# Scan of a two-block transformer kernel: exclusive cumulative sum by subtraction, transposes a step behind, weights of the later modulation scaled and added on VectorE

## The chip, the cores and the metric

The kernel runs on one core of one Trainium2 chip. A core has five engines with a queue each: TensorE (PE, with PEld for its weight loads), VectorE (DVE), ScalarE (ACT), GpSimd (POOL) and SyncE (SP), which issues most DMAs. The metric is device time in microseconds from start to end; smaller is better.

## The reference, cut to what matters

```python
def reference(...):                                   # one layer of block one, two of block two
    m_x = split(silu(c) @ mod_w + mod_b, 6)           # modulation: shifts, scales and gates, 6 x 1024
    h_x = modulate(rms_norm(x, norm1_g), m_x[0], m_x[1]);  h_c = ...           # latent and context, 256 tokens each
    z = h @ w_in                                      # r, k, v, low ranks, q, k, v, two gates
    ya = rwkv_mixer(z_c, z_x, ...)                    # the scan: both directions, 8 heads of 64
    yb = na_mixer(z_c, z_x, ...)                      # neighbourhood attention
    x = x + m_x[2] * branch_merge(z_x[9], z_x[10], ya, yb, proj_a, proj_b, w_out)
    x = x + m_x[5] * moe(modulate(rms_norm(x, norm2_g), m_x[3], m_x[4]), ...)  # 16 experts, 2 a token
    return second_block(x, ...)                       # two layers: mixer, feed-forward, gate

def rwkv_prep(...):                                   # what a step of the scan needs
    wl = w0 + tanh(lw) @ w_lora_b                     # log-decay, from a low rank
    decay = exp(-exp(-softplus(-wl) - 0.5))
    a = sigmoid(a0 + la @ a_lora_b)
    kk = normalised(k * k_k);  k_dir = k * (1 + (a - 1) * k_a)

def step(s, (w_t, k_t, v_t, kk_t, a_t, r_t)):         # over 256 context, then 256 latent tokens
    s = s * w_t - (s @ kk_t) outer (kk_t * a_t) + v_t outer k_t
    y = s @ r_t
```

## The kernel before

The work lies in stages one behind the other: norm and the first part of the modulation, input products with neighbourhood attention, the scan, the merge of both branches, the experts, and the two layers of the second block. The change is in the scan and in two things that are done beside it.

**The scan** (`rwkv`) is done in chunks of 128 tokens. Two directions, two groups of four heads and four chunks make 16 units. Three slots (`SLOTS`) take them in turn, so that slot 0 has six units and the others five. Each unit is a generator: `rwkv_prep` makes the rows of the chunk, `rwkv_chunk` makes the masked products of a chunk and calls `solve` for the triangular solve, then the state and the output are updated. Each `yield` ends a step. The function `turns` goes round all live generators and takes one step of each: three slots (each a few steps apart), `gates` (products of the gates, 160 steps), `factors` with `modulation_rest` and `bonus`, and `rwkv_out`. This round is the order in which the code is written; a scheduler then sets the order within each engine's queue, with that order as priority. Each engine takes its queue strictly from the front.

**The preparation of a unit** (`rwkv_prep`) writes `th` (tanh of decay and a), makes cumulative sums of the decay over the tokens with two products against masks of zeros and ones (`cum["i"]`, inclusive, L669; `cum["e"]`, exclusive, L670), takes exponentials of them on ACT (`pe` from the exclusive sum, `pinv` and `pi` from the inclusive one), and multiplies on DVE into the rows `rr` (L688), `nb` (L698, L699), `kh` (L703 to L705) and, in the latent chunks, `pi` (L709). `turn` transposes such a row on PE (L686, two transposes of 128x128) and copies it with ACT to `krT` or `nkT` (L687). The first use of the transposed rows is L735. The products of the solve are L835, L841 and L844, with copies `nt` on ACT (L830) and masked products `x` on DVE (L837).

**The later modulation** (`modulation_rest`): for eight blocks of 512 columns, eight pieces of `mod_w` (128x512, 256 KB each) come by DMA into `mr` (three buffers). ACT scales each with its column of silu(c) (L300), POOL adds it to `mra` (L302), and PE sums `mra` over the partitions with a column of ones (L307). Two steps lie behind each piece. DVE also makes the low parts `wl` of the gates' weights (L128).

Of the kernel before, what the change touches and what calls it, by code (L numbers as in the profile page):

```python
# [12 lines left out]
AF = mybir.ActivationFunctionType  # L13
ALU = mybir.AluOpType
# [57 lines left out]
class Kernel:  # L72
# [212 lines left out]
    def modulation_rest(self, pool):  # L285

        nc, a = self.nc, self.a
        self.rw = self.gp.tile([P, 8, 16], F32, name="rw")
        self.rbh = self.keep.tile([P, 16], F32, name="rb")
        nc.sync.dma_start(self.rw, a["router_w"].rearrange("(k p) e -> p k e", p=P))  # L290
        rb = a["router_bias"]
        nc.sync.dma_start(self.rbh, bass.AP(tensor=rb.tensor, offset=rb.offset, ap=[[0, P], [1, 16]]))
        nc.vector.tensor_scalar(self.rbh, self.rbh, 0.5, None, op0=ALU.add)
        w = a["mod_w"][0]
        for q in range(4, 12):
            acc = pool.tile([P, 512], F32, tag="mra", name="mra", bufs=1)
            for k in range(8):
                raw = pool.tile([P, 512], F32, tag="mr", name="mr", bufs=3)
                nc.sync.dma_start(raw, w[k * P:(k + 1) * P, q * 512:(q + 1) * 512])
                nc.scalar.activation(raw if k else acc, raw, AF.Copy, scale=self.sc[:, k, 0:1])  # L300
                if k:
                    nc.gpsimd.tensor_tensor(acc, acc, raw, op=ALU.add)  # L302
                yield
                yield
            ps = self.bank()
            for j in range(4):
                nc.tensor.matmul(ps[:, j:j + 1], acc[:, j * P:(j + 1) * P], self.ones, start=True, stop=True)  # L307
            nc.vector.tensor_tensor(self.m[:, q * 4:q * 4 + 4, 0], ps[:, 0:4], self.col["mod_b"][:, q * 4:q * 4 + 4],
                                    op=ALU.add)
            yield  # L310

        self.fac = self.keep.tile([P, 32], F32, name="fac")
        nc.vector.tensor_scalar(self.fac[:, 0:8], self.m[:, 16:24, 0], 0.5, None, op0=ALU.mult)
        nc.vector.tensor_copy(self.fac[:, 24:32], self.m[:, 40:48, 0])
        nc.vector.scalar_tensor_tensor(self.fac[:, 8:16], self.m[:, 32:40, 0], 1.0, self.col["norm2_g"], op0=ALU.add,
                                       op1=ALU.mult)
        nc.vector.tensor_copy(self.fac[:, 16:24], self.m[:, 24:32, 0])
        ps = self.bank()
        nc.tensor.transpose(ps[0:32, 0:P], self.fac, self.ident)
        row = pool.tile([32, P], F32, tag="mra", name="frow", bufs=1)  # L320
        nc.vector.tensor_copy(row, ps[0:32, 0:P])
        self.facrow = self.dram.tile([32, P], F32, name="facrow")
        nc.sync.dma_start(self.facrow[:, :], row)
# [163 lines left out]
    def rwkv_constants(self):  # L487
        nc, c, a = self.nc, self.rc, self.a
# [9 lines left out]
        f = lambda n: cell[0].tile([P, P], F32, name=n)  # L498
        tt, ts = nc.vector.tensor_tensor, nc.vector.tensor_scalar
        w0, w1, w2 = f("w0"), f("w1"), f("w2")  # L500
        wi0, wi1 = c.tile([P, P], I32, name="wi0"), c.tile([P, P], I32, name="wi1")
        pf, sf = f("pf"), f("sf")
# [2 lines left out]
        ts(sf, si, 0.0, None, op0=ALU.add)  # L505

        self.cum = {}
        for d, (ge_i, ge_e, half) in enumerate(((ALU.is_ge, ALU.is_gt, ALU.is_lt), (ALU.is_le, ALU.is_lt, ALU.is_ge))):
            ts(w0, pf, 64.0, None, op0=half)
            for kind, op in (("i", ge_i), ("e", ge_e)):  # L510
                m = f(f"cum{kind}{d}")
                tt(m, sf, pf, op=op)
                tt(m, m, w0, op=ALU.subtract)
                self.cum[kind, d] = m

        self.off = c.tile([P, 8], F32, name="off")
        self.offn = c.tile([P, 8], F32, name="offn")
# [10 lines left out]
        for d, (st, inc) in enumerate(((ALU.is_gt, ALU.is_ge), (ALU.is_lt, ALU.is_le))):  # L528
            m = c.tile([P, 4, P], F16, name=f"mk4{d}")
# [5 lines left out]
        for k in range(6):  # L535
# [5 lines left out]
            for d in range(2):  # L541
                m = (pf, sf)[d]
# [99 lines left out]
    def rwkv_prep(self, s, d, g, t, cur, first):  # L642

        nc, pool = self.nc, self.rp
        mm = nc.tensor.matmul
        tt, stt = nc.vector.tensor_tensor, nc.vector.scalar_tensor_tensor
# [5 lines left out]
        flat = lambda ap: ap.rearrange("p a b -> p (a b)")  # L652
# [7 lines left out]
        thw, tha = th[:, 0:256], th[:, 256:512]  # L660
# [6 lines left out]

        bi = self.bank()
        mm(bi[:, 0:256], self.cum["i", d], thw, start=True, stop=True)  # L669
        mm(bi[:, 256:512], self.cum["e", d], thw, start=True, stop=True)  # L670
        pinv, pe = tmp("pinv"), tmp("pe")
        h = -0.5 * CDEC
        nc.scalar.activation(pe, bi[:, 256:512], AF.Exp, scale=h, bias=self.off[:, 2 * d + 1:2 * d + 2])
        nc.scalar.activation(pinv, bi[:, 0:256], AF.Exp, scale=-h, bias=self.offn[:, 2 * d:2 * d + 1])
        if emit:
            pi = tmp("pi")
# [3 lines left out]
        rr, nb, kh = own([P, 2, 4, 64], "rr"), own([P, 256], "nb"), own([P, 256], "kh")  # L680
        krT, nkT = own([P, 2, 2, P], "krT"), own([P, 2, 2, P], "z0")

        def turn(src, dst):
            b = self.bank()
            for p in range(2):
                nc.tensor.transpose(b[:, p * P:(p + 1) * P], src[:, p * P:(p + 1) * P], self.ident)  # L686
            nc.scalar.activation(dst, b[:, 0:256].rearrange("p (a t) -> p a t", a=2), AF.Copy)  # L687
        tt(flat(rr[:, 0]), kk, pe, op=ALU.mult)  # L688
        turn(flat(rr[:, 0]), krT[:, :, 0, :])

        bt = self.bank()
        for p in range(2):
# [1 line left out]
        hv = self.sm.tile([P, 2, 2], F32, tag=f"hv{s}", name="hv", bufs=2)  # L694
        nc.scalar.activation(hv, bt[:, 0:4].rearrange("p (a b) -> p a b", b=2), AF.Exp, scale=h, bias=self.off64)
        yield
        u = tmp("t0")
        stt(u, tha, 1.0, kk, op0=ALU.add, op1=ALU.mult)  # L698
        stt(nb, u, -0.5, pinv, op0=ALU.mult, op1=ALU.mult)  # L699
        turn(nb, nkT[:, 0])  # L700
        yield
        u = tmp("t0")
        stt(u, tha, -1.0, self.kab[:, fs], op0=ALU.add, op1=ALU.mult)  # L703
        stt(u, u, 1.0, self.zk[t][:, fs], op0=ALU.add, op1=ALU.mult)
        tt(kh, u, pinv, op=ALU.mult)  # L705
        turn(kh, nkT[:, 1])
        yield
        if emit:
            tt(pi, self.zr[t][:, fs], pi, op=ALU.mult)  # L709
            turn(pi, krT[:, :, 1, :])  # L710
            yield
        cur.update(hv=hv, rr=rr, nb=nb, kh=kh, krT=krT, nkT=nkT)

    def rwkv_chunk(self, s, d, g, t, cur, state, i, y):
# [1520 lines left out]
```

## Time and profile before

| | |
|---|---|
| time, median of 3 runs | 1558.77 us (1555.15 to 1559.71) |
| the profiled execution | 1560.86 us |
| its span | 1559.1 us |
| PE, PEld busy | 1471.2 us (94%), 1122.8 us (72%) |
| DVE, ACT, POOL busy | 867.1 us (56%), 673.0 us (43%), 197.4 us (13%) |

Busy times are those of the span. The profiled execution is one of its own, and its time is a little above the median of the others. Lines such as L302 are lines of the kernel before.

### The profile page before, as it was taken

Reading aid. Unit: us, or ns where it says so; the run is one execution under the profiler, and the core shown is the slowest. Engines: PE = TensorE matmul, PEld = TensorE weight load, DVE = VectorE, ACT = ScalarE, POOL = GpSimd, SP = SyncE. Lnnn points to the kernel's source line nnn. Section 1 sums busy time; section 2 is a strip of 40 time slices with the busy share of each in tenths; the row PEclk is TensorE's granted clock in tenths of the full one; section 3 lists DMA queues with packets and bytes.
Section 4 is the critical chain, followed back from the end, with each engine's and each line's share of the span. In section 5 each row is a group of like instructions: output and inputs, shape, how many; then the busy total and the mean of one; then the engine's idle time right before and its main releaser. Section 6 shows DMA issues by size and latency. Waiting matters only on the chain.

```text
span 1559.1 us, 26053 instructions
## 1 busy us (share of the span) xinstructions
PE 1471.2 (94%) x10562; PEld 1122.8 (72%) x10562; DVE 867.1 (56%) x1826; ACT 673.0 (43%) x1097; POOL 197.4 (13%) x253
## 2 busy tenths in 40 slices
PE   5899999989999999789999899999999999999996
PEld 3677777878777777644443358699988887998885
DVE  3678547676666776522211245564556755755555
ACT  2433556665556553210110145554444545544443
POOL 1001123332233510058000000000000000000000
PEclk9899998898899999889999999999999999999999
DMA  9412223221222234779999925355556453555542
GB/s 326 158 46 68 68 84 116 82 82 56 68 82 83 82 119 154 306 308 420 420 419 420 393 85 187 109 188 182 181 182 202 146 189 96 175 189 189 189 162 75
DMA packets 119175, 276.29 MB, mean 177 GB/s; under 512 B 8672, under 2 KB 31876, under 8 KB 107784
## 3 DMA queue, kind: packets, MB, share of 16 engines
q1 hardware_dynamic: 115608, 270.13, 49.4%
q10 hardware_dynamic: 3407, 4.42, 0.8%
q8 instruction: 85, 1.39, 0.4%
q14 instruction: 43, 0.34, 0.1%
q0 software_dynamic: 32, 0.00, 0.0%
HBM read 272.41 MB, written 2.11 MB: 176 GB/s over the span
## 4 chain that ended last, share of the span: by engine, by line
PE 54%; DVE 1%; ACT 1%; issue 0%; DVEq 0%; ACTq 0%
PE mm L119 12%; PE mm L120 12%; PE mm L121 12%; PE mm L1546 11%; PE mm L1531 1%; PE mm L1694 1%; PE mm L1610 1%; PE mm L1951 1%; PE mm L1970 1%; PE mm L1812 1%; PE mm L1924 0%; PE mm L1980 0%; PE mm L217 0%; DVE wl L184 0%; PE mm L1913 0%
## 5 line engine op out<-in xcount | busy, mean ns | idle before, releaser
L184 DVE TENSOR_TENSOR wl<-wr,wh 128x2048 fp32r<-128x2048 f32 (+2 forms) x128 | 269.1, 2103 | 206.7 <-ACT wh L183 194.2
L183 ACT ACTIVATE wh<-wr 128x2048 fp32r<-128x2048 f32 (+2 forms) x128 | 224.9, 1760 | 156.3 <-PE mm L121 105.5
L121 PE MATMUL mm<-xTh,wl 128*128 128x256 f32 x512 | 143.9, 281 | 0.0
L120 PE MATMUL mm<-xTl,wh 128*128 128x256 f32 x512 | 143.7, 281 | 0.0
L119 PE MATMUL mm<-xTh,wh 128*128 128x256 f32 x512 | 143.3, 281 | 0.0
L119 PE MATMUL mm<-wh,fh 128*128 128x512 f32 x256 | 101.4, 396 | 0.0
L121 PE MATMUL mm<-wh,fl 128*128 128x512 f32 x256 | 101.1, 395 | 0.0
L120 PE MATMUL mm<-wl,fh 128*128 128x512 f32 x256 | 101.0, 395 | 0.0
L120 PEld LDWEIGHTS mm<-xTl,wh 128*128 128x128 f32 x512 | 96.2, 188 | 0.9 <-DVE xTl L968 0.3
L119 PEld LDWEIGHTS mm<-xTh,wh 128*128 128x128 f32 x512 | 96.1, 188 | 0.7
L119 PE MATMUL mm<-wh,xTh 128*128 128x512 f32 (+1 forms) x272 | 95.8, 352 | 0.6 <-ACT big L1888 0.4
L121 PEld LDWEIGHTS mm<-xTh,wl 128*128 128x128 f32 x512 | 96.4, 188 | 0.0
L120 PE MATMUL mm<-wl,xTh 128*128 128x512 f32 (+1 forms) x272 | 92.8, 342 | 0.0
L121 PE MATMUL mm<-wh,xTl 128*128 128x512 f32 (+1 forms) x272 | 92.6, 342 | 0.0
L302 POOL TENSOR_TENSOR mra<-mra,mr 128x512 f32<-128x512 f32 x56 | 74.3, 1327 | 54.5 <-ACT mr L300 29.6
L830 ACT ACTIVATE nt<-mm 128x512 f16<-128x512 f32 x80 | 47.2, 593 | 43.9 <-PE mm L844 38.0
L119 PEld LDWEIGHTS mm<-wh,xTh 128*128 128x128 f32 x272 | 51.2, 188 | 8.4 <-issue 0.7
L967 ACT ACTIVATE yh<-hu 128x512 fp32r<-128x512 f32 x16 | 10.1, 630 | 109.0 <-DVE hu L1602 93.8
L121 PEld LDWEIGHTS mm<-wh,fl 128*128 128x128 f32 x256 | 48.1, 188 | 11.5
L119 PE MATMUL mm<-hlh,wh 128*128 128x256 f32 x152 | 56.1, 369 | 0.0
L120 PEld LDWEIGHTS mm<-wl,fh 128*128 128x128 f32 x256 | 48.1, 188 | 10.8
L119 PEld LDWEIGHTS mm<-wh,fh 128*128 128x128 f32 x256 | 48.1, 188 | 10.7
(576 smaller groups left out, 3512.1 us busy)
## 6 DMA issues: line engine op xcount, KB each, us to landing
wr<-in_w_up_dram SPq DMA_DIRECT2D x32, 1024.0 KB, 5.7
wr<-in_w_down_dram SPq DMA_DIRECT2D x32, 1024.0 KB, 5.0
wr<-in_w_in_dram SPq DMA_DIRECT2D x22, 1024.0 KB, 5.2
wr<-in_moe_w_dram SPq DMA_DIRECT2D x21, 1024.0 KB, 13.5
wh<-in_moe_w_dram SPq DMA_DIRECT2D x20, 1024.0 KB, 13.4
wl<-in_moe_w_dram SPq DMA_DIRECT2D x20, 1024.0 KB, 14.3
mr<-in_mod_w_dram SPq DMA_DIRECT2D x64, 256.0 KB, 2.9
wx<-in_moe_w_dram SPq DMA_DIRECT2D x14, 1024.0 KB, 12.8
```

Source lines behind the costliest of these rows:

```text
L119: mm(out, l.hi, r.hi, start=start, stop=False, **kw)
L120: mm(out, l.hi, r.lo, start=False, stop=False, **kw)
L121: mm(out, l.lo, r.hi, start=False, stop=stop, **kw)
L183: self.nc.scalar.activation(w.hi, raw, AF.Copy)
L184: self.nc.vector.tensor_tensor(w.lo, raw, w.hi.bitcast(F32), op=ALU.subtract)
L302: nc.gpsimd.tensor_tensor(acc, acc, raw, op=ALU.add)
L830: nc.scalar.activation(nt, v4(bz), AF.Copy)
L1531: mm(b[:, k * 256:k * 256 + 256], part[:, t, 2 * q + k, :], sel[:, t].rearrange("p j c -> p (j c)"), start=(i == 0), stop=(i == 3))
L1546: mm(b[r], lT[:, k0 + k, c0 + SLOT * j:c0 + SLOT * j + SLOT], w[:, k], start=(start and k == 0), stop=(stop and k == n - 1))
L1610: mm(acc[2 * n + k // 2][:, k % 2], part[:, k * P:(k + 1) * P], back, start=False, stop=(g == 7 and part is y.lo), skip_group_check=True)
L1694: mm(banks[t], first[:, k, t * P:(t + 1) * P], w[:, k, :], start=(k == 0), stop=False)
L1812: nc.tensor.transpose(b[:, j * P:(j + 1) * P], self.x[:, t, 512 * n + j * P:512 * n + (j + 1) * P], self.ident)
```

## The change

Three edits. The masks of the exclusive sum and its product go; the exclusive sum of a token is the inclusive one less the token's own value, so `pe` is now the inclusive product's result minus `thw`, on DVE, and the exponential is taken in place. Each transpose (`turn`) stands one step behind the step that makes its row, and the preparation of a unit yields once more (six steps and not five; in latent chunks seven and not six). In `modulation_rest`, DVE scales a piece and adds it in one instruction; the first piece of a block is still scaled by ACT.

```diff
--- before.py
+++ after.py
@@ -297,9 +297,10 @@
             for k in range(8):
                 raw = pool.tile([P, 512], F32, tag="mr", name="mr", bufs=3)
                 nc.sync.dma_start(raw, w[k * P:(k + 1) * P, q * 512:(q + 1) * 512])
-                nc.scalar.activation(raw if k else acc, raw, AF.Copy, scale=self.sc[:, k, 0:1])
                 if k:
-                    nc.gpsimd.tensor_tensor(acc, acc, raw, op=ALU.add)
+                    nc.vector.scalar_tensor_tensor(acc, raw, self.sc[:, k, 0:1], acc, op0=ALU.mult, op1=ALU.add)
+                else:
+                    nc.scalar.activation(acc, raw, AF.Copy, scale=self.sc[:, k, 0:1])
                 yield
                 yield
             ps = self.bank()
@@ -505,13 +506,11 @@
         ts(sf, si, 0.0, None, op0=ALU.add)
 
         self.cum = {}
-        for d, (ge_i, ge_e, half) in enumerate(((ALU.is_ge, ALU.is_gt, ALU.is_lt), (ALU.is_le, ALU.is_lt, ALU.is_ge))):
+        for d, (ge_i, half) in enumerate(((ALU.is_ge, ALU.is_lt), (ALU.is_le, ALU.is_ge))):
             ts(w0, pf, 64.0, None, op0=half)
-            for kind, op in (("i", ge_i), ("e", ge_e)):
-                m = f(f"cum{kind}{d}")
-                tt(m, sf, pf, op=op)
-                tt(m, m, w0, op=ALU.subtract)
-                self.cum[kind, d] = m
+            m = self.cum["i", d] = f(f"cumi{d}")
+            tt(m, sf, pf, op=ge_i)
+            tt(m, m, w0, op=ALU.subtract)
 
         self.off = c.tile([P, 8], F32, name="off")
         self.offn = c.tile([P, 8], F32, name="offn")
@@ -667,10 +666,10 @@
 
         bi = self.bank()
         mm(bi[:, 0:256], self.cum["i", d], thw, start=True, stop=True)
-        mm(bi[:, 256:512], self.cum["e", d], thw, start=True, stop=True)
         pinv, pe = tmp("pinv"), tmp("pe")
         h = -0.5 * CDEC
-        nc.scalar.activation(pe, bi[:, 256:512], AF.Exp, scale=h, bias=self.off[:, 2 * d + 1:2 * d + 2])
+        tt(pe, bi[:, 0:256], thw, op=ALU.subtract)
+        nc.scalar.activation(pe, pe, AF.Exp, scale=h, bias=self.off[:, 2 * d + 1:2 * d + 2])
         nc.scalar.activation(pinv, bi[:, 0:256], AF.Exp, scale=-h, bias=self.offn[:, 2 * d:2 * d + 1])
         if emit:
             pi = tmp("pi")
@@ -686,7 +685,6 @@
                 nc.tensor.transpose(b[:, p * P:(p + 1) * P], src[:, p * P:(p + 1) * P], self.ident)
             nc.scalar.activation(dst, b[:, 0:256].rearrange("p (a t) -> p a t", a=2), AF.Copy)
         tt(flat(rr[:, 0]), kk, pe, op=ALU.mult)
-        turn(flat(rr[:, 0]), krT[:, :, 0, :])
 
         bt = self.bank()
         for p in range(2):
@@ -694,21 +692,24 @@
         hv = self.sm.tile([P, 2, 2], F32, tag=f"hv{s}", name="hv", bufs=2)
         nc.scalar.activation(hv, bt[:, 0:4].rearrange("p (a b) -> p a b", b=2), AF.Exp, scale=h, bias=self.off64)
         yield
+
+        turn(flat(rr[:, 0]), krT[:, :, 0, :])
         u = tmp("t0")
         stt(u, tha, 1.0, kk, op0=ALU.add, op1=ALU.mult)
         stt(nb, u, -0.5, pinv, op0=ALU.mult, op1=ALU.mult)
+        yield
         turn(nb, nkT[:, 0])
-        yield
         u = tmp("t0")
         stt(u, tha, -1.0, self.kab[:, fs], op0=ALU.add, op1=ALU.mult)
         stt(u, u, 1.0, self.zk[t][:, fs], op0=ALU.add, op1=ALU.mult)
         tt(kh, u, pinv, op=ALU.mult)
+        yield
         turn(kh, nkT[:, 1])
-        yield
         if emit:
             tt(pi, self.zr[t][:, fs], pi, op=ALU.mult)
+            yield
             turn(pi, krT[:, :, 1, :])
-            yield
+        yield
         cur.update(hv=hv, rr=rr, nb=nb, kh=kh, krT=krT, nkT=nkT)
 
     def rwkv_chunk(self, s, d, g, t, cur, state, i, y):
```

The scheduler's order changes from shortly before the scan to its end, on all engines. Behind it, the instructions stand in the same order as before. The lines of the kernel after lie one or two off those of the kernel before.

DVE's queue of the kernel before, in the seventh unit, from its row `rr` to the low part of the next gate weights:

```order
L688 TENSOR_TENSOR rr_3996<-kk,pe 128x256
L699 SCALAR_TENSOR_TENSOR nb_3997<-t_4037,pinv 128x256
L703 SCALAR_TENSOR_TENSOR t_4077<-th,kab 128x256
L704 SCALAR_TENSOR_TENSOR t_4077<-t_4077,zk 128x256
L837 TENSOR_TENSOR x_4026<-mm,lv_1173 128x256
L705 TENSOR_TENSOR kh_3998<-t_4077,pinv 128x256
L128 TENSOR_TENSOR wl<-wr,wh 128x512
```

The preparation's five instructions stand almost side by side, with one product of the solve between. The modulation's additions are on POOL and not in this queue.

The same place in the kernel after, from the subtraction that makes `pe`:

```order
L671 TENSOR_TENSOR pe<-mm,th 128x256
L854 CAST x_3922<-mm 64x256
L301 SCALAR_TENSOR_TENSOR mra<-mr,silu_c,mra 128x512
L687 TENSOR_TENSOR rr_3984<-kk,pe 128x256
L838 TENSOR_TENSOR x_4010<-mm,lv_1167 128x256
L699 SCALAR_TENSOR_TENSOR nb_3985<-t_4019,pinv 128x256
L301 SCALAR_TENSOR_TENSOR mra<-mr,silu_c,mra 128x512
L703 SCALAR_TENSOR_TENSOR t_4058<-th,kab 128x256
L301 SCALAR_TENSOR_TENSOR mra<-mr,silu_c,mra 128x512
L872 TENSOR_TENSOR rr_3247<-rr_3247,mm 128x512
L704 SCALAR_TENSOR_TENSOR t_4058<-t_4058,zk 128x256
```

Three instructions of L301, the scaled additions, now stand in this queue between `pe` and the row `kh` (L705, two rows further on), and two instructions stand between `pe` and `rr`.

PE's queue of the kernel before, at the transpose of the same unit's row `rr` (L693 is the sum over the halves of the chunk):

```order
L119 MATMUL mm<-hlh,wh 128x256
L120 MATMUL mm<-hll,wh 128x256
L121 MATMUL mm<-hlh,wl 128x256
L119 MATMUL mm<-hlh,wh 128x256
L686 MATMUL mm<-ident,rr_3996 128x128 x2
L693 MATMUL mm<-half,th 128x2 x2
L862 LDWEIGHTS x_3933
L862 MATMUL mm<-nt_3932,x_3933 64x64
```

The transpose and the sum over the halves stand side by side.

PE's queue of the kernel after, at the sum over the halves (here L691), and then at the transpose of `rr` (here L685):

```order
L845 LDWEIGHTS x_3934
L845 MATMUL mm<-nt_3888,x_3934 64x64
L120 MATMUL mm<-hll,wh 128x256
L121 MATMUL mm<-hlh,wl 128x256
L691 MATMUL mm<-half,th 128x2 x2
L119 MATMUL mm<-hlh,wh 128x256
L120 MATMUL mm<-hll,wh 128x256
L121 MATMUL mm<-hlh,wl 128x256
L863 LDWEIGHTS x_3922
```

```order
L119 MATMUL mm<-hlh,wh 128x256
L120 MATMUL mm<-hll,wh 128x256
L121 MATMUL mm<-hlh,wl 128x256
L119 MATMUL mm<-hlh,wh 128x256
L120 MATMUL mm<-hll,wh 128x256
L685 MATMUL mm<-ident,rr_3984 128x128 x2
L870 MATMUL mm<-rq_3466,tT_2094 128x128 x4
L842 LDWEIGHTS nt_3976
L842 MATMUL mm<-x_4010,nt_3976 64x64
```

The sum has kept its place behind the solve's products, and the transpose has moved back behind the next step's solve products (L863, L836) and gate products (L119 to L121): some twenty products stand between the two.

## Rows read from the trace of the kernel before

**Rows 1.** Windows: busy us (x instructions) of PE, PEld, DVE, ACT, POOL; clock, DMA share, GB/s.

```profile
0.00:220.00 220.00, 196.71 (x1137) 144.01 (x1137) 133.80 (x485) 88.74 (x168) 16.11 (x29) 0.95 0.35 118
220.00:600.00 380.00, 353.70 (x4194) 294.57 (x4194) 256.78 (x542) 216.21 (x455) 125.93 (x133) 0.92 0.32 95
600.00:1559.00 959.00, 920.81 (x5233) 684.17 (x5232) 476.54 (x801) 368.05 (x475) 55.32 (x91) 0.98 0.62 223
```

**Rows 2.** Waits of PE, 222 to 600 us: total us, times, longest.

```profile
PE mm L686 <- DVE kh L705: 8.1, 8, 1.9
PE mm L841 <- DVE x L837: 3.3, 5, 1.6
PE mm L686 <- DVE rr L688: 2.3, 5, 0.8
PE mm L686 <- DVE nb L699: 0.4, 1, 0.4
```

**Rows 3.** Groups of POOL, 220 to 600 us: count | busy us, mean ns | idle before.

```profile
L302 POOL TENSOR_TENSOR mra<-mra,mr 128x512 f32<-128x512 f32 x56 | 74.3, 1327 | 54.5 <-ACT mr L300 29.6 <-ACT mra L300 17.4 <-PE mm L852 5.7
```

**Rows 4.** Groups of ACT, 220 to 620 us.

```profile
L300 ACT ACTIVATE mr<-mr,silu_c 128x512 f32<-128x512 f32 x56 | 39.7, 718 | 20.2 <-DMA mr<-in_mod_w_dram 18.7 <-POOL mra L302 1.5
```

**Rows 5.** Groups of PE, 222 to 600 us.

```profile
L670 PE MATMUL mm<-th,cume 128*128 128x256 f32 x32 | 9.6, 382 | 0.0
```

**Rows 6.** Groups of DVE, 220 to 620 us.

```profile
L128 DVE TENSOR_TENSOR wl<-wr,wh 128x512 fp32r<-128x512 f32 x48 | 37.3, 776 | 16.4 <-ACT wh L127 15.3 <-ACT mr L300 0.7 <-issue 0.2
L703 DVE SCALAR_TENSOR_TENSOR t<-th,kab 128x256 f32<-128x256 f32 x16 | 10.6, 664 | 0.1
L699 DVE SCALAR_TENSOR_TENSOR nb<-t,pinv 128x256 f32<-128x256 f32 x16 | 9.6, 597 | 0.0
L704 DVE SCALAR_TENSOR_TENSOR t<-t,zk 128x256 f32<-128x256 f32 x16 | 9.1, 570 | 0.1
L705 DVE TENSOR_TENSOR kh<-t,pinv 128x256 f32<-128x256 f32 x16 | 8.8, 552 | 0.2
L688 DVE TENSOR_TENSOR rr<-kk,pe 128x256 f32<-128x256 f32 x16 | 7.9, 494 | 7.2 <-ACT pe L673 7.1
L837 DVE TENSOR_TENSOR x<-mm,lv 128x256 f16<-128x256 f32 x80 | 33.3, 420 | 16.6 <-PE mm L835 15.7
```

**Rows 7.** Two lines by themselves: ns shortest/median/longest, first and last start us.

```profile
L699 DVE SCALAR_TENSOR_TENSOR nb<-t,pinv x16: 407/422/1493, 229.4 to 548.2; 128x256 f32<-128x256 f32 x16
L128 DVE TENSOR_TENSOR wl<-wr,wh x48: 673/691/1768, 223.7 to 614.9; 128x512 fp32r<-128x512 f32 x48
```

**Rows 8.** Timeline of one burst: start us, us, what.

```profile
339.60 1.49 DVE L699 SCALAR_TENSOR_TENSOR nb<-t,pinv 128x256 f32<-128x256 f32 x1
342.41 2.87 POOL L302 TENSOR_TENSOR mra<-mra,mr 128x512 f32<-128x512 f32 x2
343.10 1.03 DVE L705 TENSOR_TENSOR kh<-t,pinv 128x256 f32<-128x256 f32 x1
344.06 1.77 DVE L128 TENSOR_TENSOR wl<-wr,wh 128x512 fp32r<-128x512 f32 x1
```

**Rows 9.** Windows of 10 us, columns as in the first group.

```profile
340.00:350.00 10.00, 6.60 (x97) 5.95 (x95) 9.56 (x13) 5.90 (x13) 6.40 (x6) 0.99 0.46 141
350.00:360.00 10.00, 9.06 (x61) 7.96 (x62) 4.93 (x11) 3.72 (x8) 3.32 (x4) 0.50 0.32 102
370.00:380.00 10.00, 10.00 (x123) 8.52 (x122) 5.82 (x16) 4.86 (x9) 0.97 (x2) 1.00 0.15 48
```

**Rows 10.** Waits of ACT, 222 to 600 us.

```profile
ACT mr L300 <- DMA mr<-in_mod_w_dram: 18.7, 15, 3.3
```

**Rows 11.** Waits of DVE, 222 to 600 us.

```profile
DVE rr L688 <- ACT pe L673: 7.1, 6, 1.8
```

**Rows 12.** Two lines by themselves: first and last start us close the row.

```profile
L659 ACT ACTIVATE th<-mm x16: 584/598/601, 226.7 to 544.5; 128x512 f32<-128x512 f32 x16
L880 ACT ACTIVATE rr<-mm x16: 579/598/602, 275.3 to 594.9; 128x512 f32<-128x512 f32 x16
```

## The prediction

> **What bounds the kernel now.** The order that I followed is stages first, then who waits in the stage of the change, then single instructions, since a share of busy time over 1559 us mixes stages with different limits. The change touches only the scan stage and a few constants ahead of it. In the order of instructions the two programs part shortly before the scan begins and agree again, engine by engine, behind its end, so everything from about 600 us on should only move in time. The windows by stage [rows 1] put 380 us into 220 to 600 us, which is the scan. There the PE is busy for 353.7 us (93%), the DVE for 256.8 (68%), the ACT for 216.2 (57%) and the POOL for 125.9 (33%), and the granted clock is 0.92. PE is the engine that is nearly always at something, but 93% is no proof of a full PE: a record that is stretched by the half clock or by the pipeline counts as busy too. The list of waits of PE [rows 2] tells which other engine it waits for: almost always the DVE. The largest entry is a transpose (L686) that waits for the kh row which DVE has just been told to make, 8.1 us in 8 waits; the rr and nb rows add 2.3 and 0.4. Those are 10.8 us on 14 of 56 transposes. Next comes the product L841 of the triangular solve, 3.3 us on DVE's x.
>
> The second thing to see is what the POOL does to the DVE. The 56 additions of L302 take 74.3 us of the POOL [rows 3]. In the timeline of a burst [rows 8] the two-input DVE instructions that run beside them take 1.49, 1.03 and 1.77 us, while the median of the same lines is 0.42 and 0.69 us [rows 7]. That 10 us window has DVE busy at 9.56 us and PE at only 6.60, the lowest of the scan, and in the next 10 us PE runs at a granted clock of 0.50, its lower level of 1.2 GHz [rows 9]. The bursts come once for each of the eight column blocks of the modulation.
>
> **The change part by part.** All is counted against the profiled execution: 1560.86 us, which is its span of 1559.1 us and 1.8 us around it. That run lies 2.1 us above the median of 1558.77.
>
> *Matmuls of the exclusive sum.* The 16 products of L670 go, 32 records with 9.6 us together [rows 5]. What hides work from PE here is that PE itself waits, so the gain lies between 0 and 9.6 us; PE is busy for 93%, and I take two thirds, **-6.5 us**. The four DVE instructions that built the two exclusive masks lie ahead of the scan, beside matmuls, and are costed at nothing; uncovered they would give back four times at most 0.4 us, by the median of a form twice as long [rows 7].
>
> *Transposes a step behind.* PE takes its instructions in order. Before, the transpose of a row stands in the step in which DVE makes that row; after, other products stand between them, as the order of the change shows. The bounds are 0 and the 10.8 us of [rows 2]. What is late next is the x of L841 and the masks' product L735, which come from the same DVE and ACT, so not all of it can be won. Fourteen waits of 0.8 us on average against some twenty products that now stand in between speak for most of it: **-8 us**.
>
> *ACT without the scaling.* 56 instructions of 0.718 us, 39.7 us, and 20.2 us of standing in front of them leave ACT [rows 4]; 18.7 us of the latter is a wait for the weights' DMA, with everything that ACT does for the solve queued behind it [rows 10]. The gain is between 0 and 18.7 us. ACT is idle for 43% of the stage and the waits of PE name the DVE, so I take a small value, **-2 us**. The eight scalings of the first piece stay.
>
> *DVE with scaling and adding.* The new instruction, two inputs of 128x512 in f32 and a factor for each partition, is not in the trace. The nearest row is L128 with two inputs of the same size, 0.69 us [rows 7]: 56 x 0.691 = 38.7 us. The subtraction for pe reads PSUM and SBUF at 128x256 like L837, 0.42 us [rows 6]: 16 x 0.42 = 6.7 us. Against that the stretching ends. For six lines, mean less median times count is 4.1 (L128: 48 x 0.085), 3.9, 2.8, 2.4, 2.1 and 1.2 us, together 16.5 us [rows 6, 7]. DVE thus gets 45.4 - 16.5 = 28.9 us more, 286 of 380 us, or 75%. What does the path see of it? The burst tells: before, three instructions lose 1.07 + 0.61 + 1.08 = 2.8 us there [rows 8]; in the order of the change, three additions (2.1 us) stand in the same piece, from pe to kh. So the place where PE loses most has about the same DVE load as before, and the rest of the new work falls where DVE has a quarter of its time free. Bounds: -16.5 (the stretching was all on the path, the additions lie in idle time) and +45.4 (all of it is on the path). Beside the transposes PE waits little for DVE (3.3 us for L841 [rows 2]); with DVE's idle share going from 32% to 25% such waits may double: **+3 us**.
>
> The Trainium skill, in Perfetto Trace Analysis, section Optimizing Scalar/DVE Operations, says that work can be moved off a saturated DVE to ACT or POOL, but that POOL and DVE share an SBUF read port, so that moving between those two might not help. Read backwards it speaks against expecting much of this move: by it the sum for the DVE part would be 0 and not +3, and the trace agrees in the burst (2.8 us against 2.1).
>
> *A longer way to pe.* It was product, exponential, rr; now DVE's subtraction comes ahead of the exponential. DVE already stands 7.1 us in 6 waits for the exponential in front of rr [rows 11]. In the order of the change two DVE instructions lie between pe's subtraction and rr, enough to hide an exponential on an idle ACT. Bounds 0 and 16 x 0.42 = 6.7 us; **+1 us**. Behind the waiting rr stand nb, the next addition and the solve's x.
>
> *One step more in each unit.* The preparation of a unit now yields once more. Slot 0 has six units and 159 steps, and would have 165. The scan's first unit starts its tanh at 226.7 us, the last solve ends at 594.9 [rows 12], so a step is about 368 / 159 = 2.3 us. If a step had a fixed length, six would cost 14 us; if its length is the work in it, nothing. PE is busy for 93%, so I side with the work: **+2 us**.
>
> *DMA.* The 64 loads of the weights stay with their three buffers, and no kind or number of transfer changes; on SP's queue a handful of them change places with loads for the gates. A buffer now comes free after one DVE instruction and not after one of ACT and one of POOL. Costed at nothing.
>
> The sum is -6.5 - 8 - 2 + 3 + 1 + 2 = -10.5 us, from 1560.9 to 1550 us.
>
> **The rivals.** *DVE becomes the engine that blocks (slower).* In a burst the seven additions stand within some 25 DVE instructions. Each waits in order for its DMA; ACT stood 18.7 us for the same loads [rows 10], and on DVE the solve's x, the rows of the preparation and the weights' low parts would stand behind it. With half of the 28.9 us and half of the 18.7 us on the path (+14 and +9), half of the transposes' gain (-4), and the other terms (-6.5, +1, +2), the time is about 1576 us. It decides where additions and their waits together cost the path more than 18 us. Against it: between two additions stand some four DVE instructions, and three buffers lie ahead. The skill's TensorE: Matmul & The Clock Gate, section Architectural detail, says that ACT's and DVE's queues are strictly first in, first out, which is this rival's condition; the wait of [rows 10] agrees.
>
> *Steps have a fixed length (no change).* Each slot is a chain, step behind step, and six more of them cost 10 us: -6.5 - 8 + 3 + 1 + 10, about 1560 us. For it: PE's records are stretched by waiting. Against it: three slots, the gates and the modulation overlap in each step.
>
> *The clock comes back as well (more).* The stage's clock of 0.92 costs up to 0.08 x 380 = 30 us of PE, and the falls follow bursts in which PE idles [rows 9]. If half returns, the time is about 1535 us. Against it: the bursts keep their DVE load.
>
> **How the numbers follow.** The forecast of 1550 us (its own range 1542 to 1556) has 0.48, the slower rival 0.20, no change 0.20, the clock 0.12. A measurement of this kernel can tell about 0.3%, 4.7 us, from no change: the limits are 1554.1 and 1563.4. A little of the forecast's range lies above the first. So faster has 0.57, the same 0.22, slower 0.21. The range from 1533 to 1568 us leaves out the far half of the slower rival, where the bounds of the DVE term reach, and the far part of the clock's.
>
> **What would show it.** In the scan's windows: POOL's busy time falls by about 74 us, ACT's by 40, DVE's rises by about 29 with all medians as they are and the long tails near 0.42 and 0.69 us gone. In the waits of PE: L686 behind DVE falls from 10.8 to below 4 us, and L841 and L735 don't take it over. In the waits of DVE: rr behind pe stays below 12 us, and waits for the weights' DMA stay below 8. Six steps more show as a last preparation that starts no later than now. The forecast fails if DVE's additions wait long for their DMA, if the PE's idle time moves from L686 to the next line, or if the half clock comes more often.

## The result, and the profile after

The changed kernel takes 1534.45 us (median of 4 runs, 1531.43 to 1539.16), the kernel before beside it 1559.24 us; the ratio is 0.9845 with a 95% interval of 0.9809 to 0.9882. It became faster by 24.8 us, where the forecast was 10.5. The time lies 1.5 us inside the lower end of the stated range (1533 to 1568) and outside the forecast's own (1542 to 1556); the number is that of the rival in which the clock comes back.

The windows of the profiled execution after (1536.57 us, span 1534.8), with the columns of [rows 1], and the sum over it:

```profile
0.00:220.00 220.00, 196.32 (x1151) 144.16 (x1152) 133.02 (x481) 89.14 (x169) 16.12 (x29) 0.95 0.36 120
220.00:600.00 380.00, 362.76 (x4260) 296.19 (x4259) 290.01 (x646) 191.16 (x411) 53.09 (x77) 0.96 0.33 103
sum 1560.00, PE 1455.02 PEld 1106.65 DVE 882.32 ACT 638.90 POOL 124.47; mean PE 485.01 PEld 368.88 DVE 294.11 ACT 212.97 POOL 41.49
```

Little moves ahead of 220 us (the scan's first tanh starts 2.3 us earlier). In the scan POOL goes from 125.9 to 53.1 us, ACT from 216.2 to 191.2, DVE from 256.8 to 290.0, and the granted clock from 0.92 to 0.96 [rows 1]. The scan ends earlier, so 600 us now lies deeper in the next stage; over the whole span, where this does not blur, POOL lost 72.9 us, ACT 34.1, and DVE gained 15.2 (its three windows of [rows 1] make 867.1). Busy time counts once where one record starts before the last has ended, as L128 does behind L705 in [rows 8]. Added up record by record, ACT lost 39.0 us (726.4 to 687.4) and DVE gained 25.5 (941.3 to 966.8).

The first and last tanh of a unit and the last solve, answering to [rows 12]:

```profile
L658 ACT ACTIVATE th<-mm x16: 597/598/600, 224.4 to 517.8; 128x512 f32<-128x512 f32 x16
L881 ACT ACTIVATE rr<-mm x16: 592/598/602, 273.7 to 569.3; 128x512 f32<-128x512 f32 x16
```

From first tanh to last solve it was 368.2 us and is 344.9: 23.3 of the 24.3 us between the two spans lie here. The waits of PE, answering to [rows 2], and those of DVE, to [rows 11]:

```profile
PE mm L836 <- ACT nt L831: 3.1, 7, 1.2
PE mm L842 <- DVE x L838: 2.6, 4, 0.9
PE mm L685 <- DVE kh L705: 0.2, 1, 0.2
```

```profile
DVE rr L687 <- ACT pe L672: 1.8, 3, 1.0
DVE mra L301 <- DMA mr<-in_mod_w_dram: 0.6, 2, 0.3
```

The transposes' 10.8 us are 0.2, and the solve's x (L842, L841 before) stands at 2.6 instead of 3.3. DVE waits 0.6 us for the weights' DMA, where ACT waited 18.7 [rows 10], so the slower rival has lost its condition. Groups of DVE, answering to [rows 6], and durations of two lines, to [rows 7]:

```profile
L301 DVE SCALAR_TENSOR_TENSOR mra<-mr,silu_c,mra 128x512 f32<-128x512 f32 x56 | 43.0, 768 | 3.1 <-ACT mra L303 2.3 <-DMA mr<-in_mod_w_dram 0.6
L128 DVE TENSOR_TENSOR wl<-wr,wh 128x512 fp32r<-128x512 f32 x48 | 33.7, 703 | 8.3 <-ACT wh L127 7.1 <-PE mm L121 1.1
L699 DVE SCALAR_TENSOR_TENSOR nb<-t,pinv 128x256 f32<-128x256 f32 x16 | 8.7, 546 | 0.0
L671 DVE TENSOR_TENSOR pe<-mm,th 128x256 f32<-128x256 f32 x16 | 6.8, 422 | 2.9 <-PE mm L668 2.7
```

```profile
L301 DVE SCALAR_TENSOR_TENSOR mra<-mr,silu_c,mra x56: 739/747/1219, 224.4 to 487.3; 128x512 f32<-128x512 f32 x56
L128 DVE TENSOR_TENSOR wl<-wr,wh x48: 679/686/1456, 221.9 to 591.1; 128x512 fp32r<-128x512 f32 x48
```

The new instruction has a median of 0.747 us (0.691 was taken from L128), the subtraction 0.422 (0.42 was taken). The medians of L128 and L699 stand, their means fall by 73 and 51 ns, but the tails are not gone (1.456 us at L128). Two windows of 10 us, with the columns of [rows 9]; the second answers to the first row there:

```profile
240.00:250.00 10.00, 9.25 (x79) 7.16 (x77) 6.16 (x15) 2.35 (x5) 0.45 (x1) 0.50 0.32 98
340.00:350.00 10.00, 9.98 (x108) 7.93 (x106) 8.22 (x24) 4.57 (x11) 0.39 (x1) 1.00 0.34 107
```

In the window in which PE was busy for 6.60 us it is now busy for 9.98. PE still falls to 1.2 GHz near the beginning of the scan.

### The profile page after: what moved, and what is told of

Its sections match the earlier page's. It is cut to its first block, busy times and chain, and to the rows that moved or that the text cites. A ratio compares the mean times of both kernels' runs of the same rounds, so it can differ in the third digit from the quotient of the medians.

```text
span 1534.8 us, 25869 instructions
## 1 busy us (share of the span) xinstructions
PE 1455.0 (95%) x10530; PEld 1106.7 (72%) x10530; DVE 882.3 (57%) x1894; ACT 638.9 (42%) x1041; POOL 124.5 (8%) x197
## 4 chain that ended last, share of the span: by engine, by line
PE 55%; DVE 1%; ACT 1%; issue 0%; DVEq 0%; ACTq 0%
PE mm L119 12%; PE mm L120 12%; PE mm L121 12%; PE mm L1547 12%; PE mm L1532 1%; PE mm L1611 1%; PE mm L1695 1%; PE mm L1952 1%; PE mm L1813 1%; PE mm L1971 1%; PE mm L1925 0%; PE mm L1981 0%; PE mm L217 0%; PE mm L1914 0%; DVE wl L184 0%
## 5 line engine op out<-in xcount | busy, mean ns | idle before, releaser
L121 PE MATMUL mm<-xTh,wl 128*128 128x256 f32 x512 | 143.9, 281 | 0.0
L119 PE MATMUL mm<-xTh,wh 128*128 128x256 f32 x512 | 143.2, 281 | 0.0
L119 PE MATMUL mm<-wh,fh 128*128 128x512 f32 x256 | 101.4, 396 | 0.0
L121 PE MATMUL mm<-wh,fl 128*128 128x512 f32 x256 | 101.0, 395 | 0.0
L119 PEld LDWEIGHTS mm<-xTh,wh 128*128 128x128 f32 x512 | 96.1, 188 | 0.7
L119 PE MATMUL mm<-wh,xTh 128*128 128x512 f32 (+1 forms) x272 | 95.8, 352 | 0.7 <-ACT big L1889 0.5
L121 PEld LDWEIGHTS mm<-xTh,wl 128*128 128x128 f32 x512 | 96.3, 188 | 0.0
L121 PE MATMUL mm<-wh,xTl 128*128 128x512 f32 (+1 forms) x272 | 92.5, 342 | 0.0
L119 PEld LDWEIGHTS mm<-wh,xTh 128*128 128x128 f32 x272 | 51.2, 188 | 8.5 <-ACT big L1889 0.7
L121 PEld LDWEIGHTS mm<-wh,fl 128*128 128x128 f32 x256 | 48.1, 188 | 11.5
L120 PEld LDWEIGHTS mm<-wl,fh 128*128 128x128 f32 x256 | 48.1, 188 | 10.7
L119 PEld LDWEIGHTS mm<-wh,fh 128*128 128x128 f32 x256 | 48.1, 188 | 10.6
L121 PEld LDWEIGHTS mm<-wh,xTl 128*128 128x128 f32 x272 | 51.2, 188 | 6.2
L120 PEld LDWEIGHTS mm<-wl,xTh 128*128 128x128 f32 x272 | 51.3, 188 | 6.0
```

The source lines that it names most:

```text
L119: mm(out, l.hi, r.hi, start=start, stop=False, **kw)
L120: mm(out, l.hi, r.lo, start=False, stop=False, **kw)
L121: mm(out, l.lo, r.hi, start=False, stop=stop, **kw)
```

## The experiments

M is the modulation's scaling and adding on DVE, X the exclusive sum by subtraction, T the turns a step behind with the additional step. Each kernel was timed beside the kernel before on the same chip (median 1555.52 us beside the first eight of the table, 1558.50 beside the last four).

| kernel | us, median | ratio to before (95%) | granted clock, median of its runs |
|---|---|---|---|
| before + M | 1526.96 | 0.9805 (0.9775 to 0.9835) | 0.981 |
| before + X | 1562.29 | 1.0033 (1.0014 to 1.0053) | 0.9645 |
| before + T | 1565.16 | 1.0058 (1.0035 to 1.0082) | 0.9665 |
| before + the step of T alone | 1566.67 | 1.0062 (1.0038 to 1.0086) | 0.966 |
| before + M + X | 1524.76 | 0.9805 (0.9774 to 0.9836) | 0.9795 |
| before + M + T | 1540.13 | 0.9897 (0.9866 to 0.9927) | 0.975 |
| after + 56 additions on POOL | 1570.89 | 1.0104 (1.0064 to 1.0145) | 0.9635 |
| after + 56 scalings on ACT | 1537.71 | 0.9898 (0.9863 to 0.9933) | 0.977 |
| after + 56 copies on POOL | 1545.72 | 0.9924 (0.9899 to 0.9949) | 0.972 |
| after, without the step | 1523.76 | 0.9791 (0.9766 to 0.9816) | 0.983 |
| after, with two steps | 1533.94 | 0.9856 (0.9827 to 0.9886) | 0.976 |
| after, without the step, kk on DVE | 1522.58 | 0.9781 (0.9752 to 0.9810) | 0.983 |

**The modulation alone.**

```diff
-                nc.scalar.activation(raw if k else acc, raw, AF.Copy, scale=self.sc[:, k, 0:1])
                 if k:
-                    nc.gpsimd.tensor_tensor(acc, acc, raw, op=ALU.add)
+                    nc.vector.scalar_tensor_tensor(acc, raw, self.sc[:, k, 0:1], acc, op0=ALU.mult, op1=ALU.add)
+                else:
+                    nc.scalar.activation(acc, raw, AF.Copy, scale=self.sc[:, k, 0:1])
```

> The kernel before with only the modulation's scaling and adding moved to DVE. Theory 1 (the stretching was on the path): the pairs of 1.0 to 1.8 us on DVE beside POOL's additions were what made PE idle and the clock fall; the median form of the additions adds 40 us to DVE that lie in idle time. Then this edit alone gives most of the 25 us of the whole change, -10 to -18 us, and the half clock in the scan falls from some 58 us towards 30. Theory 2 (the sum of the prediction): this edit is worth -2 + 3 = +1 us, so no difference beyond 0.3%, and the half clock stays. Theory 3 (DVE blocks when alone): without the turns a step behind, the transposes wait longer for the later kh row; +5 to +15 us, with PE's wait in L686 above 10.8 us.

It gave 28.6 us, by the medians more than the whole change and more than the 10 to 18 of theory 1; theories 2 and 3 fall. The scan's window with the sum, then a group of DVE, and lines by themselves (the last two are the first tanh and the last solve):

```profile
220.00:600.00 380.00, 361.35 (x4295) 297.92 (x4295) 288.13 (x632) 194.06 (x412) 49.77 (x65) 0.98 0.35 110
sum 1560.00, PE 1447.51 PEld 1103.58 DVE 875.56 ACT 638.87 POOL 125.02; mean PE 482.50 PEld 367.86 DVE 291.85 ACT 212.96 POOL 41.67
```

```profile
L301 DVE SCALAR_TENSOR_TENSOR mra<-mr,silu_c,mra 128x512 f32<-128x512 f32 x56 | 42.7, 762 | 1.0 <-DMA mr<-in_mod_w_dram 0.5
```

```profile
L128 DVE TENSOR_TENSOR wl<-wr,wh x48: 674/685/694, 216.9 to 577.4; 128x512 fp32r<-128x512 f32 x48
L813 DVE CAST a<-mk x32: 275/291/1066, 229.2 to 521.9; 64x256 f16<-64x256 f32 x32
L660 ACT ACTIVATE th<-mm x16: 597/597/601, 219.4 to 504.3; 128x512 f32<-128x512 f32 x16
L881 ACT ACTIVATE rr<-mm x16: 579/598/601, 259.2 to 557.4; 128x512 f32<-128x512 f32 x16
```

DVE took on 42.7 us of additions and is busy for only 8.4 us more (867.1 to 875.6). Added up record by record it is 16.7 us more (941.3 to 958.0), so 26.0 us of stretching went, where the prediction had 16.5. L128's longest instruction is 0.694 us (1.768 in [rows 7]). The clock in the scan is 0.98.

From first tanh to last solve the scan takes 338.0 us and not 368.2. That is 30.2 of the 37.9 us between the two profiled spans; another 7.3 lie ahead of the scan, where both kernels have the same instructions in the same order and the clock happened to be higher (0.97 against 0.95). So a part of the 28.6 us may not come from the edit; how large it is in the medians is not shown.

Two waits bear on this: PE's for kh here, and DVE's for POOL in the kernel before.

```profile
PE mm L687 <- DVE kh L706: 2.7, 4, 1.1
```

```profile
DVE t L698 <- POOL mra L302: 1.1, 1, 1.1
```

The second is the only wait of DVE for POOL in the scan's list, so a late kk from POOL's queue is not what M made up for.

**The subtraction alone** (the other hunks of the diff left out).

> The kernel before with only the exclusive sum by subtraction. The prediction's terms give -6.5 + 1 = -5.5 us, with 32 PE records and 9.6 us fewer. Theory 1 (the stretching was on the path) agrees or gives less, -2 to -6. A rival: pe comes later by one DVE instruction, which stands beside POOL's additions and is stretched itself, so rr's wait for pe goes from 7.1 to over 12 us and the gain is lost: 0 to +4 us.

It is 6.8 us slower, so the -5.5 falls. PE's waits in front of the transposes stay:

```profile
PE mm L684 <- DVE kh L703: 7.1, 6, 2.5
PE mm L684 <- DVE rr L686: 2.8, 4, 1.0
```

```profile
DVE rr L686 <- ACT pe L671: 2.7, 5, 1.0
```

The rival's sign, over 12 us at rr, is absent too; what the 6.8 us are is not shown.

**The turns alone.**

```diff
-        turn(kh, nkT[:, 1])
         yield
+        turn(kh, nkT[:, 1])
         if emit:
...
-            turn(pi, krT[:, :, 1, :])
             yield
+            turn(pi, krT[:, :, 1, :])
+        yield
```

> The kernel before with only the turns a step behind their rows, and the additional step in each unit. The prediction's terms give -8 + 2 = -6 us, with PE's waits in L686 from 10.8 to below 2 us. A rival (the clock hangs on these waits): with the transposes' waits gone PE does not idle, the half clock in the scan falls from some 58 to about 30 us, and this edit alone gives -15 to -20 us. Another rival: the six additional steps cost as much as the waits gave, 0 to -3 us.

It is 9.6 us slower; all three expectations miss the sign. The transposes' waits are gone, and these stand in the list in their place:

```profile
PE mm L843 <- DVE x L839: 6.7, 7, 1.8
PE mm L669 <- ACT th L659: 3.5, 3, 2.4
```

The solve's product waits 6.7 us for x (3.3 in [rows 2]), and the cumulative sum 3.5 us for the tanh (0.2 before). This execution took 1574.3 us, near the upper end of the kernel's times (1560.1 to 1576.2), so these waits may be longer than usual.

**Additions back on POOL.**

```diff
+        dm = pool.tile([P, 512], F16, tag="dm", name="dm", bufs=1)
...
+                if k:
+                    nc.gpsimd.tensor_tensor(dm, raw, raw, op=ALU.add)
```

> The changed kernel with 56 additional additions on POOL, each of the loaded weights with themselves into a scratch tile that nobody reads: POOL has its two-input work back beside DVE, while no other engine's work changes (a weight buffer is held a little longer). Theory 1 (the stretching was on the path): DVE's two-input instructions stretch again by 15 to 25 us in all, and the time goes up by 8 to 18 us. Theory 2 (the prediction counted DVE's 28.9 us more at +3): the stretching costs about a tenth of itself, 0 to +3 us. A rival: POOL holds the three weight buffers, and the additions on DVE wait for DMA by over 8 us.

The time rises by 36 us by the medians, twice what theory 1 expected, to above the kernel before. The two groups, then the scan's window and the sum over the windows:

```profile
L302 DVE SCALAR_TENSOR_TENSOR mra<-mr,silu_c,mra 128x512 f32<-128x512 f32 x56 | 52.8, 943 | 2.9 <-ACT mra L304 2.4 <-DMA mr<-in_mod_w_dram 0.4
L306 POOL TENSOR_TENSOR dm<-mr 128x512 f16<-128x512 f32 x56 | 65.0, 1161 | 77.4 <-DMA mr<-in_mod_w_dram 76.7
```

```profile
220.00:600.00 380.00, 345.75 (x4150) 282.50 (x4149) 302.12 (x612) 180.80 (x397) 117.51 (x133) 0.96 0.31 95
sum 1560.00, PE 1462.20 PEld 1110.51 DVE 912.06 ACT 638.59 POOL 188.76; mean PE 487.40 PEld 370.17 DVE 304.02 ACT 212.86 POOL 62.92
```

DVE has not one instruction more than in the changed kernel, and is busy for 29.7 us more (912.1 against 882.3; 29.0 record by record). This execution, with 1561.6 us, is the shortest of its kernel. Its span is 25.0 us longer than that of the changed kernel (1559.8 against 1534.8) at nearly the same granted clock (0.972 against 0.974, and 0.96 in both scans): in this pair, one execution of each, the stretching has its price without a change of clock. DVE's wait for the weights is 0.4 us, so the held buffers are not the cause.

**Modulation and subtraction; modulation and turns** (the changed kernel with one part undone).

> The changed kernel with the turns back at their rows and without the additional step: the modulation on DVE and the exclusive sum by subtraction. The modulation's edit alone gave -28.6 us, the whole change -24.8, the subtraction alone +7. Theory 1 (the subtraction hurt only beside POOL's additions, where pe's and rr's instructions are stretched): without them it is worth the -5.5 us of the prediction, about 1520 us. Theory 2 (it hurts by itself: pe comes one DVE instruction later and PE waits for rr and kh): about 1534 us, with the half clock in the scan above the 10 us of the modulation's edit alone. If the turns are what the whole change loses against the modulation's edit, this is at 1520 to 1527.

> The changed kernel with the exclusive sum as a product again: the modulation on DVE and the turns a step behind, with their additional step. Theory 1 (the turns a step behind and the step cost by themselves, +10 alone): about 1537 us, with the half clock in the scan above 25 us. Theory 2 (they cost only while POOL stretches DVE's rows): -6 us from the modulation's edit alone, about 1521.

Beside M the subtraction no longer costs: 1524.8 us against M's 1527.0, ratios equal. That speaks for theory 1 on the sign, but the 5.5 us are not there. The turns with their step cost M 13.2 us (1540.1 against 1527.0), which is theory 1 of that run; on M and X they cost 9.7 (the changed kernel against 1524.8). The run without X has a trace that does not help: its profiled execution lies at the lower end of its times (span 1528.5 us, clock 0.982; times from 1530.2 to 1542.95).

**The step alone, and none or two in the changed kernel.** The edits are one `yield` at the end of the preparation, added to before, taken from after, added to after.

> The kernel before with one additional step at the end of each unit's preparation and nothing else. The prediction gave the step +2 us, and up to +14 if a step has a fixed length of 2.3 us. Theory 1 (the step is what made the turns' edit slower): +8 to +14 us, the scan longer by as much. Theory 2 (a step is the work in it): 0 to +2 us, and the +10 of the turns' edit comes from where the transposes now stand.

> The changed kernel without the additional step: the last row's turn stands in the preparation's last step, and all else is as changed. Theory 1 (a step has its own price, as the run with the step alone gave +11): -10 to -13 us from the changed kernel's 1534, about 1522, with the scan shorter by as much. Theory 2 (the step is work, and the changed kernel loses against the modulation's edit through the place of the transposes): 0 to -3 us, 1531 to 1534.

> The changed kernel with one step more at the end of each unit's preparation, so two more than before. Theory 1 (a step has its own price): +8 to +13 us, about 1545, the scan longer by as much. Theory 2 (a step is the work in it): within 3 us of the changed kernel.

The step alone costs 11.2 us, as much as all of T; without it the changed kernel gains 10.7 (1534.45 to 1523.76; 8 by the ratios, whose intervals just meet). A second step costs nothing. So a step has no fixed price, and neither is its price that of work alone. The scan's windows without the step, and with two:

```profile
220.00:600.00 380.00, 366.57 (x4284) 298.08 (x4280) 296.26 (x654) 194.28 (x415) 55.85 (x73) 0.98 0.36 112
```

```profile
220.00:600.00 380.00, 361.57 (x4245) 296.81 (x4244) 288.02 (x644) 189.79 (x410) 51.41 (x77) 0.94 0.33 102
```

From first tanh to last solve the scan takes 334.9 us without the step, 344.9 with one and 348.5 in this execution with two, and 374.9 with the step alone (368.2 before). In these windows the clock is what differs most: 0.98 without the step, 0.96 with one, 0.94 in this execution with two.

**The controls: scalings on ACT, copies on POOL.** As the additions above, with `nc.scalar.activation(dm, raw, AF.Copy, scale=...)` and `nc.gpsimd.tensor_copy(dm, raw)`.

> The changed kernel with 56 additional scalings on ACT, from the loaded weights into a scratch tile that nobody reads: ACT has its 40 us back and the weight buffers are held a little longer, as in the run with additions on POOL, and POOL stays empty. Theory 1 (what POOL's additions cost came from sharing with DVE): 0 to +4 us, and DVE's medians and means as in the changed kernel. A rival (what counts is the additional instructions, the held buffers or ACT's load): +15 us or more, as a large part of the +36 us of POOL's additions.

> The changed kernel with 56 additional copies on POOL, from the loaded weights into a scratch tile that nobody reads: as the run with additions, but with one input. Theory 1 (it is POOL's two-input work that stretches DVE's): DVE's means stay near those of the changed kernel, scaled additions below 0.80 us, and the time rises by 0 to 5 us. Theory 2 (any work of POOL on SBUF does it): the scaled additions go above 0.85 us and the time rises by over 12 us; the run with additions had 0.94 us and +36 us.

The scalings cost 3.3 us by the medians (some 8 by the ratios, whose intervals overlap with that of the changed kernel), with the buffers held and 40.4 us of scalings on ACT. So a part of the 36 us, at most some 8, is not POOL's. The copies cost 11.3 us (12.3 by the ratios). The scaled additions beside the scalings (first row) and beside the copies:

```profile
L302 DVE SCALAR_TENSOR_TENSOR mra<-mr,silu_c,mra 128x512 f32<-128x512 f32 x56 | 44.4, 793 | 2.3 <-ACT mra L304 1.8 <-DMA mr<-in_mod_w_dram 0.3
```

```profile
L302 DVE SCALAR_TENSOR_TENSOR mra<-mr,silu_c,mra 128x512 f32<-128x512 f32 x56 | 47.4, 846 | 2.8 <-ACT mra L304 2.4 <-DMA mr<-in_mod_w_dram 0.2
L306 POOL CAST dm<-mr 128x512 f16<-128x512 f32 x56 | 41.1, 733 | 89.3 <-DMA mr<-in_mod_w_dram 86.5 <-PE mm L658 2.2
```

The copies' 0.846 us is just below the 0.85 of theory 2, and their time lies above theory 1 and at the edge of theory 2: POOL work with one input stretches DVE too, but less.

**The rest of POOL's pairs on DVE.** `eng = nc.vector` for kk in every unit, on top of the kernel without the step.

> The changed kernel without the additional step and with the other regular two-input work of POOL in the scan, the two instructions that make kk in 12 of 16 units, on DVE too. Theory 1 (POOL's two-input work costs the path more than DVE's additional busy time): the 24 instructions add about 10 us to DVE at 0.42 us each, some 8 us of stretching go, and the time is 2 to 6 us below the run without the step, near 1518. Theory 2 (DVE is full enough now, or kk on DVE stands in front of rows that PE waits for): 0 to +6 us from that run.

It gave 1.2 us, less than this measurement can tell. The kernel without the step (1523.76 us) and this one (1522.58) are faster than the changed kernel by the medians; so is M with X.

## Why the prediction was right, and where it was wrong

The direction held, and the stated range by 1.5 us. The sum did not: -10.5 against -24.8, from parts that were wrong in opposite ways and on a mechanism that the forecast had priced at next to nothing. That the time lies inside the range is in part luck: without the extra step it would have been 1523.76 us, outside it.

*DVE with scaling and adding* (+3) is the term that failed, in sign and size. M alone is this term and the one for ACT, together forecast at +1, and it gave -28.6 us. What DVE's time adds up to was nearly right: record by record the whole change adds 25.5 us, where the prediction had 28.9. The stretching that M took away was larger than forecast, 26.0 us and not 16.5. The six lines of the prediction gave 12.9 of it, and lines outside the six nearly all the rest: the cast L812 5.4 us, the kk that DVE makes itself 3.1, L629 2.1, L698 1.1. In the kernel before (shortest/median/longest):

```profile
L812 DVE CAST a<-mk x32: 275/394/1626, 239.4 to 562.3; 64x256 f16<-64x256 f32 x32
L629 DVE TENSOR_TENSOR sbd<-sbd,hv x24: 274/289/1351, 300.7 to 551.1; 64x128 f32<-64x128 f32 x24
L698 DVE SCALAR_TENSOR_TENSOR t<-th,kk x16: 424/426/1123, 227.3 to 545.2; 128x256 f32<-128x256 f32 x16
L709 DVE TENSOR_TENSOR pi<-zr,pi x8: 413/830/953, 383.6 to 548.5; 128x256 f32<-128x256 f32 x8
L837 DVE TENSOR_TENSOR x<-mm,lv x80: 406/424/426, 245.9 to 587.2; 128x256 f16<-128x256 f32 x80
```

L812, the line that gained most, has one input. L837, with one input in PSUM, is never stretched. L709 shows how a median misleads: a line that is nearly always stretched hides it there (0.830 us; its shortest is 0.413). But it is as long with M (median 0.830 us), and short only when kk leaves POOL as well, as the run with kk on DVE has it:

```profile
L709 DVE TENSOR_TENSOR pi<-zr,pi x8: 409/418/419, 358.6 to 510.8; 128x256 f32<-128x256 f32 x8
```

So POOL's kk stretches it and not the additions, and no part of M's gain lies there.

The step that failed is the price on the path: "the place where PE loses most has about the same DVE load as before" counted microseconds alike. M gave 28.6 us where 26.0 us of stretching went and 42.7 us of additions came, so what went was worth about its own length (the clock's part included), and what came cost next to nothing. The latter follows from the sum alone; that the additions fell into idle time of DVE, while the stretched pairs came where a unit's rows were due, is argued and not shown. That the stretching was on the path is shown from the other side by the additions on POOL: 29.7 us of it put back cost 25.0 us in the profiled pair at nearly the same clock. By the medians it is 36 us, some 13 of them clock by the slope below (0.976 to 0.9635).

The Trainium skill's page SBUF — State Buffer, section SBUF: two separate sides, has a rule on who can be hit, without a cost: DVE and GpSimd share one pair of ports as an exclusive lock, and a DVE instruction takes it in a 2-port mode, or with two SBUF inputs, then only against a GpSimd instruction that reads SBUF. The runs agree on L698 (hit) and L837 with its PSUM input (not hit), and on one-input copies of POOL counting too; in which mode the cast L812 ran, no run shows. The prediction read the Trainium skill's page Perfetto Trace Analysis, section Optimizing Scalar/DVE Operations, as a sum of 0 for DVE; the page says only that such a move might not help, and the run of M alone decides against that use of it.

*ACT without the scaling* (-2): the scalings put back on ACT cost 3.3 us by the medians. The term is of the right size, or a few us small.

*Transposes a step behind* (-8): the mechanism is right (10.8 to 0.2 us of waits), the price is not. T without its step is worth -1.5 us on the kernel before (1565.16 - 1566.67) and -1.0 on M and X (1523.76 - 1524.76), both less than these runs can tell from nothing. A wait of PE is not time on the path when the next product stands for the same engine: in the run of T alone x and th took it over. Beside M alone the transposes' waits for kh were down to 2.7 us without any turn moved.

*Matmuls of the exclusive sum and the longer way to pe* (-6.5 + 1): +6.8 alone, -2.2 beside M, -5.7 beside M and T (1534.45 - 1540.13). The size was right only in company.

*One step more* (+2): +11.2 alone, 10.7 in the changed kernel, 0 for a second one. The rival "steps have a fixed length" had the first price (10 us) and the wrong reason. Why the first step costs and the second does not stays open; a step at another place was not tried.

*The clock* (its rival, 0.12) is a part of the result and not the larger one. In the profiled pair half of the scan's clock came back, 0.92 to 0.96, which is 0.04 x 380 = 15 us and what that rival had. But the profiled execution before, with a mean clock of 0.964, lies low among the 47 others of this kernel, which go from 0.962 to 0.974 with a median of 0.970. Over these the time went with the clock by 10.6 us for 0.01 (correlation -0.86). By this slope M's gain is some 11 us of clock (0.971 to 0.981) and 18 of the rest; the changed kernel's 24.8 are some 6 (0.970 to 0.976) and 18.5; the step in the changed kernel (0.983 to 0.976) is 7 of its 10.7. This split is an estimate: a slope within one kernel is carried to others, and a correlation does not say whether the clock made the time or PE's idle time made both. How the clock fell before reads as in [rows 9]: stretched rows, PE busy for 6.60 of 10 us, then 1.2 GHz.

The sum of the parts by themselves is -28.6 + 6.8 + 9.6 = -12.2 us, the whole is -24.8. The difference is X, which costs 6.8 us beside POOL's additions and gains 2.2 to 5.7 without them. T costs about the same in both: 9.6 alone, 13.2 beside M, 9.7 beside M and X. The way M, X, T gives -28.6 - 2.2 + 9.7 = -21.1 us; the 3.7 us left lie between the medians of the kernel before beside M (1555.52) and beside the changed kernel (1559.24).

## What to carry to other kernels

Work moved from POOL to DVE is to be costed by what it frees: sum each DVE line against its shortest instruction, not its median, over all lines, casts with one input included, and look at who waits for them. In the scan (220 to 620 us) that sum is 41 us before and 17 with M; it is an upper bound, since POOL's other work goes on stretching DVE. A list of waits names candidates; only what no later instruction takes over is time. Each part of a change deserves its own run: here one part gave as much as the whole, and one `yield` took some 10 us back (8 by the ratios).

## What the runs showed of the hardware that was not expected

56 additions of POOL with 65.0 us made DVE busy for 29.7 us more, 0.46 us for each us of POOL; 56 copies with 41.1 us for 12.2 us more (894.5 against 882.3), 0.30; record by record it is 29.0 and 10.4 us, 0.45 and 0.25. ACT's 40.4 us beside the same buffers did it by 3.1 us (885.4). The whole-program sums of the last two:

```profile
sum 1560.00, PE 1462.48 PEld 1111.47 DVE 894.51 ACT 638.43 POOL 163.84; mean PE 487.49 PEld 370.49 DVE 298.17 ACT 212.81 POOL 54.61
```

```profile
sum 1560.00, PE 1448.10 PEld 1100.20 DVE 885.44 ACT 670.20 POOL 126.65; mean PE 1448.10 PEld 1100.20 DVE 885.44 ACT 670.20 POOL 126.65
```

An f32 instruction with two 128x512 inputs and a factor for each partition takes 0.747 us (median of L301), 0.06 more than one without the factor (L128, 0.686).
